# A hybrid encoder layer: the first token mixer's softmax is divided by its sums after the value product instead of before

## The chip, the cores and the metric

The kernel runs on one core of a Trainium2 chip. The metric is the device time of one execution in microseconds (us). Five engines of the core work side by side, each with its own instruction stream: TensorE (PE; the loading of its stationary operand is listed as PEld), VectorE (DVE), ScalarE (ACT), GpSimd (POOL) and SyncE (SP), which here only issues DMAs. 16 DMA engines move data between HBM and the on-chip SBUF. PSUM, where the matrix products land, has eight banks of 128 x 512 float32.

## The reference

One encoder layer on a sequence of 512 tokens of width 1024, everything in float32:

```
proj  = h @ w_in                                   # queries, keys, values of both mixers
o_a   = windowed_gqa_sink(qa, ka, va, a_sink)      # mixer A: 16 query heads, 4 key heads, |i-j| <= 128
o_b   = dilated_mixture(qb, kb, vb)                # mixer B: 3 groups (window, dilation) x 4 heads
g_a, g_b = split(sigmoid(h @ w_gate + b_gate))
mixed = g_a * (o_a @ w_br_a) + g_b * (o_b @ w_br_b)
h     = layer_norm(alpha * h + mixed @ w_out)
f     = (silu(h @ w_ff_gate) * (h @ w_ff_up)) @ w_ff_down
h     = layer_norm(alpha * h + f)
```

What matters here is mixer A. For each block of 128 queries and each head, with a learned logit `sk` beside the scores:

```
m   = max(sc.max(-1), sk)
p   = exp(sc - m)
den = p.sum(-1) + exp(sk - m)
o   = (p @ v) / den
```

The division by `den` may come before or after the product with `v`; the result is the same up to rounding.

## The kernel before

**Numbers as pairs.** A float32 operand is split into a rounded high part (a float32r copy) and a low part (the difference). A product of two split operands takes three matmuls: high by high, high by low, low by high. The high part is made by a copy on ACT or DVE (`copy`, line 387 on ACT, line 389 on DVE), the low part by a subtraction on DVE (mostly lines 413 and 558).

**Weights.** All weight matrices are packed into "units" of 128 x 1024, fetched as two halves of 128 x 512 (256 KB) into SBUF slots, mostly by SP (line 395). A unit that is used alone (`unit`, two calls of `half_unit`) takes 8 x 3 matmuls with 512 moving columns (`feat_k`, lines 537 to 539). Two units can be computed together by `pair_x`: seven products of half size in place of eight, by sums and differences of the weight halves (`S1` to `S4`) and of the input (`x_forms`). Each product is 12 matmuls with 256 moving columns (`product`, lines 659 to 661). Two of the sums of a pair (`S1`, `S3`) are made by a second DMA of POOL that adds into the first (line 401), two (`S2`, `S4`) on DVE, or by a DMA when the pair is written `D:`. The kernel before has 13 pairs.

**Scheduling.** The program is written as a list of operations with priorities. A planner inside the kernel (`Program.run`) plays the engines forward with costs of its own, and issues for each engine the ready operation with the lowest priority number whose buffers fit. So the order of the instructions on each engine is fixed when the program is built; on the chip, semaphores keep the dependencies and every engine works its list in order. The string `ORDER` names the steps of the first half: `X` the forms of the input, `q2` or `k1` a unit of queries or keys of mixer A, `VA` its values, `P:a,b` and `D:a,b` a pair, `R` and `r` the rotary turn of the rows waiting for it, `A0` to `A3` the four key heads of mixer A, `V0`, `V12`, `Q..`, `K..` and `B0` to `B3` the parts of mixer B, `g` a gate unit, `O` the fetch of one eighth of mixer A's result. The number behind `@` moves a step's priorities earlier (negative) or later.

**Mixer A.** `unit_a(g, b, ...)` does one key head `g` and one block `b` of queries, four heads at a time, 16 calls in all. For each head: two matmuls for the scores (lines 903 and 904), mask and maximum on DVE (line 1067), the exponential on ACT with the sum of the row (line 1071). Then DVE takes the reciprocal of the four sums (line 1074), and `normalise` multiplies each head's probabilities, 128 queries x 256 or 384 keys, by the reciprocal of its row: on ACT (line 1006) or on DVE (line 1008), whichever the planner has free. The probabilities are transposed by PE (line 1018) and multiplied with the values (lines 1084 and 1085). The result, head channels as rows and queries as columns, is stored to DRAM (`oaD`, line 1091) as two parts that must be added.

**The way back.** `fetch_oa(k)` (lines 1371 and 1372) loads the first part by SP and adds the second part by a POOL DMA, and `split_of` splits the sum (lines 1351 and 1357). There are eight such tiles; the first four put their high part in a slot, the others in a buffer of the class `x4` that has held the input (`N_XA = 4`).

**The branch stage.** After the steps of `ORDER`, a fixed list `BRANCHES` gives the order of eight products with `w_br_a` (`branch_a`, 24 matmuls each) and eight with `w_br_b` (`branch_b`). Then come the product with `w_out` (lines 1549 to 1551) with the first layer norm, the feed-forward part (lines 1759 to 1761 and 1970 to 1972) and the last layer norm.

Of the kernel before, what the change touches and what calls it, by code (L numbers as in the profile page):

```python
# [52 lines left out]
SPARE, SPARE2 = (4, 12)  # L53
# [48 lines left out]
PAIR_DMA = ()  # L102


BRANCHES = "a0 a1 a2 a3 a4 b0 a5 b1 b2 a6 b3 b4 a7 b5 b6 b7"
# [32 lines left out]
class Program:  # L138


    def __init__(self, limits):
# [7 lines left out]
        self.rooms = {}  # L149
# [5 lines left out]
    def op(self, alts, fn, reads=(), writes=(), prio=0.0, after=(), abs_prio=None, moves=0.0, extra=0, table=None):  # L155
# [30 lines left out]
        return o  # L186

# [19 lines left out]
    def run(self):  # L207
# [27 lines left out]
        while n_left:  # L235
# [13 lines left out]
            while progress:  # L249
                progress = False  # L250
                for e in engines:
# [19 lines left out]
                    for b in o.bufs:  # L271
                        if b.tile is None:
                            if b.keys[0] in self.rooms:
                                b.room = self.rooms[b.keys[0]].popleft()
# [70 lines left out]
def hybrid_layer(ctx: ExitStack, tc: tile.TileContext, wpack, xT, xtok, sink, bgate,  # L345
# [146 lines left out]
    for j in range(2):  # L492
        for w, u in (("k", U_KA), ("q", U_QA), ("v", U_VA), *((i, U_GATE + 8 + i) for i in range(N_ALONG))):
# [114 lines left out]
    def pair_x(ua, ub, by_dma=False):  # L608
# [3 lines left out]
        W, A = {}, {}  # L612

# [145 lines left out]
    def in_sbuf(u):  # L759

        ps, t = bank("dense"), slot()
        feat_x(ps, unit(u))
# [286 lines left out]
    obT = [slot(F32, "res") for _ in range(2)]  # L1049

    def unit_a(g, b, qs, kk, vs):
# [6 lines left out]
        for h in range(4):  # L1058
# [15 lines left out]
        op([(DVE, 0.08)], lambda e: nc.vector.reciprocal(st.t[:, 8:12], st.t[:, 4:8]),  # L1074
           reads=[(st, "l", h) for h in range(4)], writes=[(st, "r")])
        for h in range(4):
            normalise(lambda h=h: ps_[h].t[:, :n], ps_[h], n, lambda h=h: st.t[:, 8 + h:9 + h], (st, "r"))
# [205 lines left out]
    def gate_of(f, t):  # L1283
# [3 lines left out]
        if f in AWAY:  # L1287
            put_away(f)
# [6 lines left out]
    def gate(f, ps=None):  # L1295
# [8 lines left out]
        if f in AWAY:  # L1304
# [11 lines left out]

    psk, psq, psv = bank("dense"), bank("dense"), bank("dense")
# [12 lines left out]
    for f in range(N_ALONG):  # L1330
        gate(8 + f, ps=along[f])
    ka, qa = {0: k_near(psk, 4)}, {0: q_near(psq, 4, (0, 0))}
# [782 lines left out]
```

## Time and profile before

| | us |
|---|---|
| median of three runs | 724.5 (724.41 to 724.72) |
| the profiled execution | 724.82, of which 723.0 are the span of the instructions |
| PE busy | 712.5 |
| PEld busy | 667.2 |
| DVE busy | 664.4 |
| ACT busy | 494.6 |
| POOL busy | 173.2 |

The granted clock of TensorE is full speed all through. By the lines of PE's matmuls, the first products (five units beside each other, then one alone) run from 4 to 37 us, mixer A's scores appear from 64 to 236 us, mixer B's from 235 to 309 us, the branch stage begins at 301 us, the product with `w_out` at 362 us and the feed-forward part at 406 us. The last matmul ends at 716 us. PE's busy time overlaps in itself, since matmuls are pipelined: what one matmul costs is read from the distance of the starts.

### The profile page before, as it was taken

To read this page: it belongs to the slowest core of one execution; us is meant where nothing else is said; L and a number is where in the kernel's file an instruction comes from. 1 tells how busy PE (TensorE), PEld (TensorE's weight loads), DVE (VectorE), ACT (ScalarE), POOL (GpSimd) and SP (SyncE) were. 2 spreads that over 40 slices of the span, in tenths; PEclk is the share of its full clock that TensorE was granted. 3 is DMA by queue.
4 is the path that set the end of the run, shared out by engine and by line. 5 is a ranking of instruction groups with operands and counts; after the bars stand their busy time and mean duration, and the time that the engine had idled before them with its cause. 6 is when DMAs were issued, how large, how long until landed. Compare 5 with 4: busy or idle time off the path is not lost.

```text
span 723.0 us, 14810 instructions
## 1 busy us (share of the span) xinstructions
PE 712.5 (99%) x4947; PEld 667.2 (92%) x4947; DVE 664.4 (92%) x1425; ACT 494.6 (68%) x1136; POOL 173.2 (24%) x347
## 2 busy tenths in 40 slices
PE   8999999999999999999999999999999999999996
PEld 6889999998999998988888999999999999999985
DVE  6998999999999989999958998999999999999987
ACT  5768889889878997767625666756567566666821
POOL 0113343322423591550020022121121201212000
PEclk9999999999999999999999999999999999999999
DMA  8978967887568789766690499776897868979402
GB/s 257 294 215 210 235 168 213 227 216 179 137 169 204 187 255 253 219 196 219 199 210 33 110 300 232 177 203 165 238 238 197 223 164 219 253 196 194 106 29 88
DMA packets 81275, 141.44 MB, mean 196 GB/s; under 512 B 11024, under 2 KB 15760, under 8 KB 81200
## 3 DMA queue, kind: packets, MB, share of 16 engines
q1 hardware_dynamic: 63472, 107.07, 46.3%
q0 software_dynamic: 17456, 33.30, 26.6%
q8 instruction: 39, 0.64, 0.4%
q14 instruction: 36, 0.29, 0.1%
q10 hardware_dynamic: 272, 0.13, 0.1%
HBM read 119.69 MB, written 8.39 MB: 177 GB/s over the span
## 4 chain that ended last, share of the span: by engine, by line
PE 90%; DMA 4%; DVE 3%; SPq 2%; ACT 1%; issue 0%; POOL 0%; DVEq 0%; ACTq 0%; POOLq 0%
PE ps L1761 10%; PE ps L1759 10%; PE ps L1760 9%; PE ps L659 5%; PE ps L661 5%; PE ps L660 5%; PE ps L537 4%; PE ps L538 4%; PE ps L539 4%; PE ps L1970 4%; PE ps L1972 4%; PE ps L1971 4%; PE ps L1018 3%; DMA sl<-wpack 3%; PE ps L1549 3%; PE ps L1551 3%
## 5 line engine op out<-in xcount | busy, mean ns | idle before, releaser
L387 ACT ACTIVATE sl<-sl 128x512 fp32r<-128x512 f32 (+3 forms) x457 | 253.8, 588 | 60.7 <-DVE sl L558 43.3
L558 DVE TENSOR_TENSOR sl<-sl,sl 128x512 fp32r<-128x512 f32 (+3 forms) x415 | 245.3, 628 | 6.0 <-ACT sl L387 5.0
L387 ACT ACTIVATE sl<-ps 128x256 f32<-128x256 f32 (+6 forms) x214 | 88.5, 440 | 76.6 <-PE ps L1761 53.0
L401 POOL DMA_DIRECT2D sl<-wpack x70 | 63.0, 931 | 319.1 <-DMA sl<-wpack 92.0
L1760 PE MATMUL ps<-sl,sl 128*128 128x256 f32 x352 | 96.8, 275 | 0.0
L1761 PE MATMUL ps<-sl,sl 128*128 128x256 f32 x352 | 96.8, 275 | 0.0
L1759 PE MATMUL ps<-sl,sl 128*128 128x256 f32 x352 | 96.8, 275 | 0.0
L1759 PE MATMUL ps<-x,sl 128*128 128x256 f32 x264 | 72.6, 275 | 0.0
L1760 PE MATMUL ps<-x,sl 128*128 128x256 f32 x264 | 72.6, 275 | 0.0
L1761 PE MATMUL ps<-x,sl 128*128 128x256 f32 x264 | 72.6, 275 | 0.0
L1759 PEld LDWEIGHTS ps<-sl,sl 128*128 128x128 f32 x352 | 67.6, 192 | 0.1
L1760 PEld LDWEIGHTS ps<-sl,sl 128*128 128x128 f32 x352 | 67.6, 192 | 0.1
L1761 PEld LDWEIGHTS ps<-sl,sl 128*128 128x128 f32 x352 | 67.6, 192 | 0.0
L537 PE MATMUL ps<-x,sl 128*128 128x512 f32 (+1 forms) x161 | 62.1, 386 | 0.7 <-ACT x L387 0.7
L539 PE MATMUL ps<-x,sl 128*128 128x512 f32 (+1 forms) x161 | 60.9, 378 | 0.0
L659 PE MATMUL ps<-sl,sl 128*128 128x256 f32 x208 | 57.8, 278 | 0.9 <-ACT sl L667 0.9
L661 PE MATMUL ps<-sl,sl 128*128 128x256 f32 x208 | 57.3, 276 | 0.0
L660 PE MATMUL ps<-sl,sl 128*128 128x256 f32 x208 | 57.2, 275 | 0.0
L558 DVE TENSOR_TENSOR sl<-sl,ps 128x512 f32<-128x512 f32 (+1 forms) x72 | 47.3, 661 | 9.0 <-PE ps L1972 5.8
L1759 PEld LDWEIGHTS ps<-x,sl 128*128 128x128 f32 x264 | 50.6, 192 | 0.4
L1760 PEld LDWEIGHTS ps<-x,sl 128*128 128x128 f32 x264 | 50.6, 192 | 0.4
L1761 PEld LDWEIGHTS ps<-x,sl 128*128 128x128 f32 x264 | 50.7, 192 | 0.0
(174 smaller groups left out, 2006.6 us busy)
## 6 DMA issues: line engine op xcount, KB each, us to landing
sl<-wpack SPq DMA_DIRECT2D x254, 256.0 KB
sl<-wpack POOLq DMA_DIRECT2D x70, 256.0 KB, 5.5
wf<-wpack SPq DMA_DIRECT2D x51, 256.0 KB
sl<-sl SPq DMA_DIRECT2D x56, 128.0 KB
wf<-wpack POOLq DMA_DIRECT2D x24, 256.0 KB, 5.3
oa<-sl POOLq DMA_DIRECT2D x32, 128.0 KB, 3.6
sl<-sl SPq DMA_DIRECT2D x72, 32.0 KB
gz<-sl SPq DMA_DIRECT2D x8, 256.0 KB
```

The lines of the kernel that those rows point to most:

```text
L387: nc.scalar.activation(dst, src, AF.Copy)
L401: op([(POOL, 1.0)], lambda e: nc.gpsimd.dma_start(b.t, src2, accum_op=ALU.add), reads=[b], writes=[b], prio=prio, moves=1.65)
L537: mm(o, a, x0, start=(k == 0 and begins), stop=False, skip_group_check=split)
L538: mm(o, a, x1, start=False, stop=False, skip_group_check=split)
L539: mm(o, b, x0, start=False, stop=(k == nk - 1), skip_group_check=split)
L558: op([(DVE, dve(w))], lambda e: nc.vector.tensor_tensor(dst(), x(), y(), op=o), reads=reads, writes=writes, prio=prio)
L659: mm(o, wh, pairs(bh[k]()), start=(first and k == 0), stop=False, skip_group_check=True)
L660: mm(o, wh, pairs(bl[k]()), start=False, stop=False, skip_group_check=True)
L661: mm(o, wl, pairs(bh[k]()), start=False, stop=(k == 3), skip_group_check=True)
L1759: mm(o, wh, pairs(bh[k]()), start=(first and k == 0), stop=False, skip_group_check=True)
L1760: mm(o, wh, pairs(bl[k]()), start=False, stop=False, skip_group_check=True)
L1761: mm(o, wl, pairs(bh[k]()), start=False, stop=(k == 3), skip_group_check=True)
```

## The change

- In `unit_a` the reciprocals go into one tile `rall` (128 x 64: 16 columns for each block, four for each key head), and the four `normalise` operations are gone. The probabilities go on unnormalised.
- `sums_in_rows`, called by the first `O`, transposes `rall` with PE, four transposes of 128 x 16, so that each of the 16 heads becomes a row of 512 queries; copies the 16 rows out of PSUM and stores them to DRAM (`rD`).
- `fetch_oa` loads for each of its tiles two of these rows, each spread over 64 partitions by its DMA, into a slot `fac`, and multiplies the fetched tile by it on DVE before the split.
- `ORDER` has one more pair (`P:g,g`), 14 in all, for two gate units that were computed alone. The steps are in another order with other numbers; the first query and key units' rotation (`q0`, `k0`), which followed the first products directly, and the branch products (`a0` to `b7`, behind the mark `/`) are now steps of it. `BRANCHES` is gone.
- All eight high parts of `fetch_oa` go into slots (`N_XA = 8`). Some offsets change (`FORMS`, `VAL`, `OA_AFTER`, the reserve `SPARE`), and banks of PSUM for the class `d` are chosen by what they held before (`room_for`).
- `BY_DMA` and `PAIR_DMA`, lists of weight halves whose low part a DMA makes, get entries.

```diff
-SPARE, SPARE2 = (4, 12)
+SPARE, SPARE2 = (8, 12)
...
 ORDER = """
-X@-11 VA@-23 q2@-799 q1@-877 P:q3,g@-124 R@-106 D:k1,q4@-31 R@155 P:q5,Q01@-843 A0@-168 D:q6,q7@-47 D:g,g@-34 r@631 P:g,Q00@-22 L@-4 A2@-96
-D:g,K00@-31 A1@-48 R@187 V12@-20 P:g,K01@-67 R@-5 P:Q02,K02@-28 A3@-55 V0@55 R@5 B0@-7 B1@11 O@25 O@35 P:K10,Q10@-39 O@-13 O@-54 K11@-34 R@24
-O@11 P:Q12,Q11@-30 g@28 K12@-12 O@950 g@25 r O@43 P:g,g@-2 B2@-525 O@-304 B3@21 g@-29 P:g,g@-32 g@-8
+q0@-19 q1@-890 X@-157 P:q3,g@-307 R@78 k0@-34 D:k1,q4@-107 R@-5 VA@-216 q2@-427 A0@-228 P:q5,Q01@-811 D:q6,q7@-199 r@1495 D:g,g@-109
+P:g,Q00@-48 L@-92 D:g,K00@-19 A1@-71 V12@-11 R@-15 A3@-63 P:g,K01@-97 R@-22 A2@-343 P:Q02,K02@-13 r@-291 V0@25 B0@-44 O@-320 P:K10,Q10@-13
+K11@-37 O@-29 B1@-2 R@532 O@9 O@31 P:Q12,Q11@-8 P:g,g@-7 K12@-35 P:g,g@-24 O@-546 r g@-24 O@-7 B2@-572 O@-29 B3@-377 P:g,g@-42 O g@4 /@49
+a3@-30 a0@-14 a1@-22 a2@-53 b0@11 a4@-50 a5@-26 a6@8 b3@14 b1@-67 b2@-31 b4@38 a7@-39 b7@-16 b6@33 b5
 """
-FORMS = -255.0
-VAL = 140.0
-OA_AFTER = (1, 0, 0, 0, 0, 1, 0, 0)
+FORMS = -315.0
+VAL = 110.0
+OA_AFTER = (0, 0, 0, 1, 0, 0, 0, 0)
...
-STORE, OA, OA_SPLIT, OB_SPLIT, N_OA, N_XA = 0.0, -60.0, -140.0, -140.0, 4, 4
+STORE, OA, OA_SPLIT, OB_SPLIT, N_OA, N_XA = 0.0, -60.0, -140.0, -140.0, 4, 8
-BY_DMA = ()
+BY_DMA = [(14, 1), (31, 0), (38, 0), (45, 1), (64, 1)]
-PAIR_DMA = ()
+PAIR_DMA = [(15, 'A12')]
-BRANCHES = "a0 a1 a2 a3 a4 b0 a5 b1 b2 a6 b3 b4 a7 b5 b6 b7"
+GATES = (8, 9, 10, 11, 12, 13, 14, 15, 0, 1, 2, 3, 4, 5, 6, 7)
...
+    def room_for(self, b):
+        free = self.rooms[b.keys[0]]
+        if b.keys[0] != "bank":
+            return free.popleft()
+        room = next((r for r in free if self.whole.get(r)), free[0]) if b.keys[1] == "d" else free[0]
+        free.remove(room)
+        self.whole[room] = b.keys[1] in ("dense", "o", "d", "dff")
+        return room
...
     def half_unit(u, j):
-        if j == 1 and u in BY_DMA:
+        if (u, j) in BY_DMA:
...
+        nth = env["pairs"]
+        env["pairs"] += 1
...
-            if key in PAIR_DMA:
+            if (nth, key) in PAIR_DMA:
...
+    rall = fixed([P, 64], "rall")
+    rD = Buf("dram", None, lambda: dram.tile([16, S], F32, name=name("rD")))
+
+    def sums_in_rows():
+        pb, rows = bank("tb"), slot()
+        def go(e):
+            for b in range(NR):
+                nc.tensor.transpose(pb.t[0:16, b * P:(b + 1) * P], rall.t[:, 16 * b:16 * b + 16], ident.t)
+        op([(PE, 0.436)], go, reads=[ident, *[(rall, g, b) for g in range(4) for b in range(NR)]], writes=[pb])
+        op(cp_alts(S, True), lambda e: copy(e, rows.t[0:16], pb.t[0:16]), reads=[pb], writes=[rows])
+        op([(SP, 0.1)], lambda e: nc.sync.dma_start(rD.t, rows.t[0:16]), reads=[rows], writes=[rD])
+        env["rows"] = True
...
     def unit_a(g, b, qs, kk, vs):
-        op([(DVE, 0.08)], lambda e: nc.vector.reciprocal(st.t[:, 8:12], st.t[:, 4:8]),
-           reads=[(st, "l", h) for h in range(4)], writes=[(st, "r")])
-        for h in range(4):
-            normalise(lambda h=h: ps_[h].t[:, :n], ps_[h], n, lambda h=h: st.t[:, 8 + h:9 + h], (st, "r"))
+        c = 16 * b + 4 * g
+        op([(DVE, 0.08)], lambda e: nc.vector.reciprocal(rall.t[:, c:c + 4], st.t[:, 4:8]),
+           reads=[(st, "l", h) for h in range(4)], writes=[(rall, g, b)])
...
-    ka, qa = {0: k_near(psk, 4)}, {0: q_near(psq, 4, (0, 0))}
+    ka, qa = {}, {}
...
     def fetch_oa(k):
+        if "rows" not in env:
+            sums_in_rows()
...
+        fac = slot()
+        for i in range(2):
+            op([(SP, 0.365)], lambda e, i=i: nc.sync.dma_start(
+                fac.t[64 * i:64 * i + 64], rD.t[2 * k + i].partition_broadcast(64)), reads=[rD], writes=[(fac, i)], prio=OAP[k // 4])
+        op([(DVE, dve(S))], lambda e: nc.vector.tensor_tensor(st.t, st.t, fac.t, op=ALU.mult),
+           reads=[st, (fac, 0), (fac, 1)], writes=[st], prio=OA_SPLIT)
...
     def step(w):
+        elif w == "/":
+            late()
+        elif w[0] in "ab":
+            branch(w)
+        elif w in first_of:
+            first_of[w][1](first_of[w][0], False)
...
-    sa.extend(fetch_oa(k) for k in range(len(sa), 8))
-    MA = moving(sa)
+    def late():
+        op([(POOL, 0.0)], free_all, after=lasts)
+        sa.extend(fetch_oa(k) for k in range(len(sa), 8))
+        MA.extend(moving(sa))
+        env["late"] = True
```

More of the change, by code (lines that the diff above doesn't have):

```diff
@@ L1286, in gate_of @@
             t.t, t.t, AF.Tanh, bias=bg.t[:, f:f + 1], scale=0.5), reads=[(t, 1), (t, 2), bg], writes=[t], prio=EV)
-        if f in AWAY:
+        if f in AWAY and not env["late"]:
             put_away(f)
@@ L1303, in gate @@
            reads=[ps, bg], writes=[t], prio=EV)
-        if f in AWAY:
+        if f in AWAY and not env["late"]:
             put_away(f)
@@ L1315, in dense_k @@
         return k_post(ps, nt) if nt else k_pairs(ps)
+    env = {"pairs": 0, "gate": N_ALONG, "turn": [], "qs": {}, "ks": {}, "late": False}
     psk, psq, psv = bank("dense"), bank("dense"), bank("dense")
@@ L1449, in step @@
                 op([(POOL, 0.0)], lambda e: pr.limits.update(ROOMS[hs]), after=list(exps))
-    for w in ORDER.split():
-        w, _, later = w.partition("@")
-        pr.T += float(later or 0)
-        step(w)
-        pr.T -= float(later or 0)
     def free_all(e):
@@ L1459, in free_all @@
         pr.spare = SPARE2
-    op([(POOL, 0.0)], free_all, after=lasts)
     def moving(parts):
@@ L1507, in branch_b @@
         return mark
-    names = BRANCHES.split()
-    marks = []
-    for n, w in enumerate(names):
-        k = 8 + int(w[1])
-        if w[0] == "b":
-            if k in away:
-                fetch_gate(k, [*exps, marks[names.index("b%d" % (k - 11))]] if k > 10 else exps)
-        marks.append((branch_a if w[0] == "a" else branch_b)(int(w[1])))
-    for w, mark in zip(names, marks):
-        env[w] = [mark]
+    for w in ORDER.split():
+        w, _, later = w.partition("@")
+        pr.T += float(later or 0)
+        step(w)
+        pr.T -= float(later or 0)
     xt = {(t, j): slot() for t in range(NR) for j in range(2)}
```

47 lines of the change are left out of this document (31 added, 16 removed).

## The prediction

> **What bounds the kernel now.** I read the page's busy times first, then PE's waits, then the starts of single matmuls.
>
> ```profile
> span 723.0 us, 14810 instructions
> ...
> PE 712.5 (99%) x4947; PEld 667.2 (92%) x4947; DVE 664.4 (92%) x1425; ACT 494.6 (68%) x1136; POOL 173.2 (24%) x347
> ...
> q1 hardware_dynamic: 63472, 107.07, 46.3%
> q0 software_dynamic: 17456, 33.30, 26.6%
> ```
> ```profile
> PE ps L473 <- DVE eps L524: 1.2, 1, 1.2
> PE ps L659 <- ACT sl L667: 0.9, 1, 0.9
> PE ps L537 <- ACT x L387: 0.7, 1, 0.7
> PE ps L1018 <- ACT sl L1006: 0.4, 1, 0.4
> ```
>
> PE waits four times, 3.2 us in all. The first and third waits (1.2 + 0.7) are the start of the program, which the diff leaves alone. What an edit of the first half can win by removing waits is 0.9 + 0.4 = 1.3 us; all else must come from fewer or shorter matmuls. The timeline gives the price of a matmul, first and last row of two undisturbed stretches:
>
> ```profile
> 364.66 0.38 PE L1551 MATMUL ps<-sl,sl 128*128 128x512 f32 x1
> ...
> 372.00 0.38 PE L1549 MATMUL ps<-sl,sl 128*128 128x512 f32 x1
> ```
> ```profile
> 424.78 0.28 PE L1761 MATMUL ps<-sl,sl 128*128 128x256 f32 x1
> ...
> 431.93 0.28 PE L1759 MATMUL ps<-sl,sl 128*128 128x256 f32 x1
> ```
>
> 35 rows, 34 steps: 7.34 / 34 = 0.216 us for 512 columns. 65 rows, 64 steps: 7.15 / 64 = 0.1117 us for 256 columns. The tail behind the last matmul is the last layer norm, which the change doesn't touch.
>
> **The change on PE.** One more pair: 7 x 12 x 0.1117 = 9.38 us in place of two units of 24 matmuls, 48 x 0.216 = 10.37 us: -0.99 us. The other 13 pairs are there before. The reciprocals' transposes are four, and the identity streams 128 columns in each, as in mixer A's own transposes, of which the chain of waits shows eight in a row:
>
> ```profile
> 85.44 0.87 PE ps L1018 x8
> ```
>
> 4 x 0.87 / 8 = +0.44 us. Sum on PE: -0.55 us. Order on PE costs nothing as long as nothing is waited for.
>
> Against the pair speaks a rule of the Trainium skill (Perfetto Trace Analysis, section Identifying the Most-Contended Engine): matmul busy time is a poor measure of headroom, and the busy share of the weight loads is to be used. A pair has 84 loads in place of 48. If loads set the pace, the pair would lose, which is the last rival below. The steps of 0.1117 us, each with its own load, speak against it here.
>
> **What falls away on ACT and DVE.** The normalising of mixer A, 32 instructions of 384 and 32 of 256 columns; the 256 rows hold 24 of mixer B too, which stay:
>
> ```profile
> L1006 ACT ACTIVATE sl<-sl,st 128x256 f32<-128x256 f32 x32 | 14.6, 497 | 2.2 <-DVE st L1074 2.2
> L1006 ACT ACTIVATE sl<-sl,st 128x384 f32<-128x384 f32 x19 | 10.7, 609 | 0.0
> L1008 DVE TENSOR_SCALAR sl<-sl,st 128x256 f32<-128x256 f32 x24 | 7.7, 348 | 0.1
> L1008 DVE TENSOR_SCALAR sl<-sl,st 128x384 f32<-128x384 f32 x13 | 5.4, 431 | 0.1
> L558 DVE TENSOR_TENSOR sl<-sl,sl 128x512 f32<-128x512 f32 x66 | 45.0, 685 | 0.5
> ```
>
> With 32 of 56 shared as the whole is, ACT loses 19 x 0.609 + 18 x 0.497 = 20.5 us and DVE 13 x 0.431 + 14 x 0.348 = 10.5 us, all between 64 and 236 us. PE has no wait in that stretch (the 0.9 comes at 42 us, the 0.4 at 279 us), so I cost this relief at nothing; its cover is PE's own queue of matmuls. The reciprocals stay, 16 as before.
>
> **What is added later.** Eight multiplications of 128 x 512 on DVE, 8 x 0.685 = 5.5 us, and the pair's extra splits: seven weight tiles in place of four and two sums, 5 x 0.685 = 3.4 us. These 8.9 us fall mainly into 250 to 340 us, where `O` and the pairs of gates stand in `ORDER`. DMA gets 16 loads of 128 KB, which is 2.1 MB. By the page's queue rows a plain MB costs 0.463 x 723 / 107.07 = 3.1 us of all 16 engines, an added-up MB 0.266 x 723 / 33.30 = 5.8 us. So the rows cost 6.6 us, and the pair (five plain loads for four and two adding ones, 0.26 MB each) 0.8 + 3.0 = 3.8 us. The windows of that stretch (PE, PEld, DVE, ACT, POOL busy, clock, DMA share, GB/s):
>
> ```profile
> 250.00:300.00 50.00, 49.60 (x331) 45.57 (x330) 44.37 (x113) 39.30 (x106) 25.35 (x69) 1.00 0.91 241
> 300.00:340.00 40.00, 40.00 (x225) 35.98 (x224) 37.25 (x103) 28.67 (x74) 16.51 (x63) 1.00 0.65 210
> ```
>
> DVE has 90 - 81.6 = 8.4 us free in these 90, DMA 50 x 0.09 + 40 x 0.35 = 4.5 + 14 = 18.5. The additions fit or nearly so if the order spreads them, so I take 0. Ends: -0.4 us (PE's fourth wait, at 279 us, goes) and +5.9 us (the DMA rival).
>
> SP gets 17 more issues, and each waits in its list: the loads of the rows for the one store of `rD`, behind which queue the weight loads that SP issues next. The nearest row for such a trip through DRAM is a 128 KB store, 3.6 us from issue to landing. Weight tiles loaded ahead cover it; without them PE would wait those 3.6 us, less than the DMA rival's 5.9. POOL gets the pair's two adding DMAs; it is busy 25.35 of 50 and 16.51 of 40 us there, so 0. The copy of the 16 rows out of PSUM is one instruction on ACT, which has 22 us free in these 90.
>
> ```profile
> oa<-sl POOLq DMA_DIRECT2D x32, 128.0 KB, 3.6
> ```
>
> **The first pair's wait.** The chain of waits leading to the 0.9 us:
>
> ```profile
> 34.81 0.63 DVE sl L558
> 35.45 0.72 DVE sl L774
> 36.17 0.57 DVE sl L772
> 36.74 1.20 DVE sl L558 x2
> 37.94 0.54 DVE sl L772
> 38.48 0.73 DVE sl L774
> 39.20 0.56 DVE sl L558
> 39.77 0.60 DVE sl L776
> 40.37 0.61 DVE sl L558
> 41.07 0.65 ACT sl L387
> ...
> 43.13 0.28 ACT sl L667
> ```
>
> Lines 772 to 776 rotate the first query and key units. They stand before the forms that the pair needs, 3.2 of DVE's 6.2 us; ACT waits for the last form, with the eviction of line 667 behind it in its list, and PE waits for that. In the change `q0` and `k0` are steps of their own, `k0` behind a pair, and the forms are more urgent (`FORMS` and `X`). The same forms, the same loads and the same in-order lists remain, though, and a second pair is pulled nearer. Ends: -0.9 (gone) and +0.9 (twice). As half of DVE's stretch is the rotation, I take half the wait: -0.45.
>
> **Edits at no cost.** The new entries of `BY_DMA` and `PAIR_DMA` reach nothing: units 14, 31 and 45 are computed in pairs, 38 in the first products, 64 in the feed-forward part, none by `half_unit`; and pairs count from 0 to 13, so there is no 15. The four high parts moved into slots no longer wait for the input's buffers; PE has no wait where those are read (40.00 busy of 40 from 300 on), so 0, and if the eight slots of rows and four of parts crowd out loads, it is the DMA rival again. The choice of banks and the order of the branches fall where PE shows no wait either: 0.
>
> **Sum.** 724.8 (the profiled execution) - 0.55 - 0.45 = 723.8. The profiled one lies 0.3 above the median of the three runs, so 723.5 by the median.
>
> **The rivals.** 0.2%, about what a measurement of this kernel can tell from no change, is 1.45 us: under 723.05 is faster, over 725.95 slower.
>
> *Both waits go and none comes:* -0.55 - 0.9 - 0.4 = -1.85, so 722.6, or a little lower with the small starts of PE's switches. For it: the relief before 236 us leaves room to prepare the later pairs early. Against: the wait at 279 us is for line 1006 of mixer B, which stays.
>
> *DMA is late at the fetches (slower):* from 250 to 300 us 4.5 us are free, and 6.6 + 3.8 = 10.4 us of transfers come in. If nothing of it moves behind 300 us, 5.9 us stay over, and branch products or the last pairs wait for rows or weights. It decides from 0.55 us seen by PE on, where the gain of the pair is spent; half of the overflow is +3.0: 724.5 - 0.55 + 3.0 = 727.0. For it: the chain to the wait at 279 us already begins with a fetch, `oa`, of 6.4 us, and a row move behind it.
>
> ```profile
> 261.01 6.40 DMA sl<-oa
> 267.43 3.51 DMA sl<-sl
> ```
>
> Against: those 14 us from 300 on, and `fetch_oa` may start after `B0` rather than `B1`.
>
> *DVE becomes the bound from 250 to 340 us:* 8.9 us against 8.4 free is an overflow of 0.5; with the first wait unchanged 724.5 - 0.55 + 0.5 = 724.4.
>
> *Weight loads set the pace:* the pair costs 84 x 0.192 = 16.1 us by PEld's durations, 5.8 above the 10.37, so 724.5 + 5.8 + 0.4 = 730.7.
>
> ```profile
> L661 PEld LDWEIGHTS ps<-sl,sl 128*128 128x128 f32 x208 | 39.9, 192 | 0.1
> ```
>
> **How the numbers follow.** The sum of small terms (half the first wait) 0.33, both waits gone 0.36, DVE 0.13, DMA 0.16, weight loads 0.02. The first and third stay within 0.2%, less some spread to either side; the second is faster; the last two are slower. That gives 0.38 faster, 0.44 the same, 0.18 slower. Low end: 722.3, the second case with a start or two less. High end: 726.0, into the DMA case (1.5 us seen by PE), leaving about one in ten above it.
>
> **What would show it.** Lines 659 to 661 with 392 matmuls each rather than 364, spaced as before, and four transposes more. Lines 1006 and 1008 with 32 instructions left in all, those of mixer B. PE's list of waits without the 0.9 or with it halved. In the windows from 250 to 340 us, DMA near full before 300 and DVE near full throughout; PE under its 49.60 and 40.00 would speak for the DMA or the DVE rival, and its releaser tells which. A multiplication waiting long for its row, with branch matmuls behind it, would make the prediction wrong; so would a wait of several us anywhere in the first 340.

## The result, and the profile after

| | median, us | ratio to before, 95% interval |
|---|---|---|
| before, 20 executions beside the change | 724.71 (723.97 to 725.79) | |
| changed, 20 executions | 731.57 (726.46 to 739.27) | 1.0086 (1.0067 to 1.0106) |

Two of the 20 executions (738.34 and 739.27 us) are in a slow state; without them the median is 731.08 us, and the ratios and all comparisons below leave such executions out. The change makes the kernel slower by 0.9%; by these medians it is 6.4 us. The prediction, 723.5 in a range of 722.3 to 726.0, missed. The kernel before repeats within 1.8 us; the other 18 executions of the changed one spread over 8.6 us. The profiled execution of the changed kernel is the quickest of its 20 (726.46 us), so its page shows the least of what went wrong, and I read a second profile of the same kernel (732.31 us) beside it.

The page of the changed kernel: span, busy times, DMA queues, and the shares of the chain that ended last.

```profile
span 724.6 us, 14933 instructions
...
PE 713.0 (98%) x4987; PEld 668.1 (92%) x4987; DVE 662.1 (91%) x1406; ACT 485.8 (67%) x1112; POOL 167.6 (23%) x349
...
q1 hardware_dynamic: 65056, 109.60, 48.1%
q0 software_dynamic: 17744, 33.83, 26.8%
...
PE 84%; DMA 7%; DVE 4%; SPq 2%; ACT 2%; issue 1%; POOL 0%; DVEq 0%; ACTq 0%
```

ACT has 8.8 us less to do and DVE 2.3 us less, and the time is longer all the same: neither was what PE waited for. DMA's share of the chain is now 7% (4% before). PE's waits (line waited at, what it waited for, us in total, times, longest):

```profile
PE ps L483 <- DVE eps L534: 1.2, 1, 1.2
PE ps L1280 <- DVE sl L978: 1.1, 1, 1.1
PE ps L671 <- ACT sl L679: 1.0, 2, 0.6
PE ps L1677 <- DVE sl L1659: 0.6, 1, 0.6
PE ps L1237 <- ACT sl L1020: 0.2, 1, 0.2
```

The lines have moved by 10 to 47: 671 is the pairs' product (659 before), 1020 the normalising on ACT, now of mixer B alone (1006), 1677 the transposes behind the first layer norm. New are the second row, a product of mixer B (line 1280) that waits for the split of its values (line 978), the fourth, and the small fifth. The two windows that the prediction quoted, now of the changed kernel (us, busy PE, PEld, DVE, ACT, POOL, clock, DMA share, GB/s):

```profile
250.00:300.00 50.00, 48.62 (x334) 44.81 (x334) 46.30 (x104) 39.58 (x93) 18.12 (x37) 1.00 0.94 249
300.00:340.00 40.00, 40.00 (x231) 36.11 (x230) 36.99 (x108) 28.90 (x80) 17.23 (x68) 1.00 0.75 226
```

PE lost 1.4 us before 300, and DMA is busier there, 0.94 against 0.91. Where the 1.1 us come from is in the chain of waits (start, us, what):

```profile
266.56 8.72 DMA sl<-wpack
275.30 0.54 SPq L766
275.88 3.86 DMA sl<-sl
...
281.70 6.02 DMA sl<-wpack
287.74 0.63 ACT sl L397
...
290.77 0.61 ACT sl L397
...
293.07 0.60 DVE sl L1410
...
294.28 0.34 DVE sl L978
294.75 0.75 PE ps L1280 x4
```

The chain follows a weight load (`wpack`) of 8.7 us, a rotary move of SP, and another weight load of 6.0 us. Then ACT makes high parts one after another, DVE has the multiplication by the rows (line 1410) and the split of mixer B's values behind them, and PE waits for that split. The first weight load of the chain has this ahead of it in SP's list (timeline of SP, start, us):

```profile
235.20 2.45 SPq L1408 DMA_DIRECT2D sl<-rD  x4
...
238.81 0.45 SPq L1408 DMA_DIRECT2D sl<-rD  x1
...
239.94 1.09 SPq L1408 DMA_DIRECT2D sl<-rD  x2
...
241.71 1.08 SPq L1408 DMA_DIRECT2D sl<-rD  x2
...
243.48 0.44 SPq L1408 DMA_DIRECT2D sl<-rD  x1
...
259.04 5.52 SPq L1408 DMA_DIRECT2D sl<-rD  x6
...
266.00 0.97 SPq L405 DMA_DIRECT2D sl<-wpack  x2
```

Line 1408 is the row load. A row of this view runs from the start of its first issue to the end of its last, so the sixteen take up 2.45 + 0.45 + 1.09 + 1.08 + 0.44 + 5.52 = 11.0 us of SP's list. 8.0 us of it are the issues themselves, 0.44 to 0.59 us each; the rest is waiting between them, 2.6 us in the row of the last six alone. The weight load at 266.0 is the next load of weights behind them.

What the issues wait for is in SP's own waits, from 230 to 310 us:

```profile
SPq L856 <- DMA sl<-wpack: 5.0, 5, 1.6
SPq L766 <- DMA sl<-wpack: 1.8, 1, 1.8
...
SPq L1408 <- DMA sl<-wpack: 1.6, 2, 1.0
```

A row load reads nothing of a weight load. But in the trace the 569 DMAs of SP report their landing by eight semaphores in fixed turn, and 554 of them wait, before they are issued, for the semaphore that they are to use. So an issue stands still until the DMA eight issues ahead of it has landed: the last six row loads wait in this way for three weight loads and one fetch, 2.4 us.

The second profile of the same kernel, 732.31 us, has the same wait, longer; its waits, and its windows at the place:

```profile
PE ps L1280 <- DVE sl L978: 3.7, 1, 3.7
```
```profile
280.00:300.00 20.00, 16.27 (x100) 14.51 (x99) 16.47 (x35) 14.38 (x33) 3.48 (x4) 1.00 0.87 242
300.00:340.00 40.00, 40.00 (x215) 35.72 (x214) 35.24 (x104) 26.10 (x72) 17.25 (x68) 0.96 0.77 228
```

PE stands still for 3.7 us, and after that the granted clock is 0.96 over 40 us, 1.6 us more. Over the 18 executions the mean clock falls from 0.998 (726.46 us) to 0.992 (735.07 us); (1 - clock) x time grows from 1.5 to 5.9 us, so by this estimate some 4.4 of the 8.6 us of spread are clock, and the rest would be the waiting itself.

### The profile page after: what moved, and what is told of

Same layout as the page of the kernel before. It is cut to its first block, busy times and chain, and to the rows that moved or that the text cites. A ratio compares the mean times of both kernels' runs of the same rounds, so it can differ in the third digit from the quotient of the medians.

```text
span 724.6 us, 14933 instructions
## 1 busy us (share of the span) xinstructions
PE 713.0 (98%) x4987; PEld 668.1 (92%) x4987; DVE 662.1 (91%) x1406; ACT 485.8 (67%) x1112; POOL 167.6 (23%) x349
## 4 chain that ended last, share of the span: by engine, by line
PE 84%; DMA 7%; DVE 4%; SPq 2%; ACT 2%; issue 1%; POOL 0%; DVEq 0%; ACTq 0%
PE ps L1807 10%; PE ps L1808 9%; PE ps L1806 9%; DMA sl<-wpack 5%; PE ps L671 4%; PE ps L672 4%; PE ps L673 4%; PE ps L2017 4%; PE ps L2019 4%; PE ps L2018 4%; PE ps L547 3%; PE ps L549 3%; PE ps L548 3%; PE ps L1032 3%; PE ps L1598 3%; PE ps L1596 3%
## 5 line engine op out<-in xcount | busy, mean ns | idle before, releaser
L397 ACT ACTIVATE sl<-sl 128x512 fp32r<-128x512 f32 (+3 forms) x468 | 259.2, 589 | 57.7 <-DVE sl L568 35.3
L568 DVE TENSOR_TENSOR sl<-sl,sl 128x512 fp32r<-128x512 f32 (+3 forms) x424 | 252.2, 629 | 8.0 <-ACT sl L397 7.0
L397 ACT ACTIVATE sl<-ps 128x256 f32<-128x256 f32 (+7 forms) x215 | 89.8, 440 | 78.1 <-PE ps L1808 50.7
L411 POOL DMA_DIRECT2D sl<-wpack x72 | 66.1, 938 | 312.5 <-DMA sl<-wpack 84.9
L1807 PE MATMUL ps<-sl,sl 128*128 128x256 f32 x352 | 96.8, 275 | 0.0
L1808 PE MATMUL ps<-sl,sl 128*128 128x256 f32 x352 | 96.8, 275 | 0.0
L1806 PE MATMUL ps<-sl,sl 128*128 128x256 f32 x352 | 96.8, 275 | 0.0
L671 PE MATMUL ps<-sl,sl 128*128 128x256 f32 x224 | 62.3, 278 | 1.0 <-ACT sl L679 1.0
L672 PE MATMUL ps<-sl,sl 128*128 128x256 f32 x224 | 61.6, 275 | 0.0
L673 PE MATMUL ps<-sl,sl 128*128 128x256 f32 x224 | 61.6, 275 | 0.0
L423 DVE TENSOR_TENSOR sl<-sl,sl 128x512 fp32r<-128x512 f32 x70 | 46.6, 682 | 2.4 <-ACT sl L397 2.4
L2017 PE MATMUL ps<-sl,sl 128*128 128x512 f32 x126 | 47.8, 380 | 0.0
```

The source lines that it names most:

```text
L397: nc.scalar.activation(dst, src, AF.Copy)
L411: op([(POOL, 1.0)], lambda e: nc.gpsimd.dma_start(b.t, src2, accum_op=ALU.add), reads=[b], writes=[b], prio=prio, moves=1.65)
L423: op([(DVE, dve(S))], lambda e: nc.vector.tensor_tensor(l.t, src.t, f32(h.t), op=ALU.subtract), reads=[src, h], writes=[l], prio=prio, abs ...
L568: op([(DVE, dve(w))], lambda e: nc.vector.tensor_tensor(dst(), x(), y(), op=o), reads=reads, writes=writes, prio=prio)
L671: mm(o, wh, pairs(bh[k]()), start=(first and k == 0), stop=False, skip_group_check=True)
L672: mm(o, wh, pairs(bl[k]()), start=False, stop=False, skip_group_check=True)
```

## The experiments

Theory A, the rival of the prediction: the sixteen row loads make DMA late between 240 and 300 us, by their bytes (2.1 MB). Theory B: the new order itself is at fault. Theory C came up on the way: the number of issues is the price, whatever they move. In the table "row loads" are those of line 1408; each ratio is to the kernel before on the same chip at the same time. The kernels without row loads, with short rows and with loads from the weights do not compute the layer: mixer A's factors are left out or wrong in them.

| kernel | row loads | median, us | before, us | ratio, 95% interval |
|---|---|---|---|---|
| changed, a second time | 16 of 128 KB | 731.24 | 724.72 | 1.0080 (1.0055 to 1.0105) |
| no row loads | none | 725.81 | 724.72 | 1.0016 (1.0003 to 1.0030) |
| short rows | 16 of 4 KB | 727.60 | 724.50 | 1.0046 (1.0018 to 1.0075) |
| from the weights, one row repeated | 16 of 128 KB | 729.18 | 724.50 | 1.0069 (1.0043 to 1.0095) |
| from the weights, plain | 16 of 128 KB | 731.08 | 724.50 | 1.0098 (1.0070 to 1.0126) |
| the same, every second partition | 16 of 128 KB | 731.82 | 724.49 | 1.0096 (1.0079 to 1.0113) |
| from the weights, one load a tile | 8 of 256 KB | 726.40 | 724.43 | 1.0023 (1.0011 to 1.0036) |
| the change with one load a tile | 8 of 256 KB | 727.04 | 724.49 | 1.0036 (1.0023 to 1.0049) |
| the same, issued by POOL | 8 of 256 KB | 728.73 | 724.43 | 1.0063 (1.0051 to 1.0076) |
| the change, loads issued by ACT | 16 of 128 KB | 733.36 | 724.27 | 1.0125 (1.0106 to 1.0144) |
| before, with 16 extra copies | 16 copies of 128 KB | 729.25 | 724.27 | 1.0068 (1.0052 to 1.0084) |
| before, with 16 short copies | 16 copies of 4 KB | 728.48 | 724.43 | 1.0057 (1.0045 to 1.0070) |

Below, "over before" is the median less that of the kernel before in the same row, and two kernels are compared by it.

### The changed kernel again, twice

> The changed kernel as it is, once more, for a profile of another execution: the one shown (726.5 us) is the fastest of its executions, the median is 731.6 us. Row theory (the fetches with their 16 row loads make DMA late from 240 to 300 us): an execution near 731 us shows PE waits of some 4 to 6 us more in 240 to 300 us than the fast one, the releasers ending in landings of weights or of the result's fetch. Order theory (the new order of the first steps leaves too little time for landings, the rows are innocent): the additional waits lie before 240 us, above all at 40 to 65 us.

> The changed kernel once more, for the profile of another execution (median 731.6 us, from 726.5 to 739.3). Traffic theory: where the execution is some us slower than the 726.5 us shown, PE's additional waits lie between 240 and 340 us, with landings of DMAs in the chain before them, and a wait near 3 us or more is followed by a lower granted clock. Order theory: they lie at 40 to 65 us and at 400 us.

731.24 us, 6.5 over before, against 731.08 at first; the single execution gave 732.31 and the second profile shown above. The loss comes back. The profile of the first of these two runs is of its quickest execution (727.43 us), and the wait at line 1280 is 0.3 us there, so it shows little of the loss.

### Without the row loads

```diff
-            op([(SP, 0.365)], lambda e, i=i: nc.sync.dma_start(
-                fac.t[64 * i:64 * i + 64], rD.t[2 * k + i].partition_broadcast(64)), ...
+            op([(SP, 0.365)], lambda e, i=i: None, ...
-        ... nc.vector.tensor_tensor(st.t, st.t, fac.t, op=ALU.mult)
+        ... nc.vector.tensor_tensor(st.t, st.t, st.t, op=ALU.mult)
```

> The changed kernel with the same instruction order, but without the 16 row loads of fetch_oa; the fetched tile is multiplied with itself, so the results of mixer A are left out of their scale. Row theory: 2.1 MB less (6.6 us of all DMA engines) in the stretch where DMA is full; the median falls to 724 to 726 us and the spread shrinks to about 2 us. Order theory: the median stays at 729 to 732 us with a spread of several us.

1.1 us over before, where the change is 6.4: 5.3 us are gone with the order and all multiplications left as they are. Its window has no gap left:

```profile
250.00:300.00 50.00, 50.00 (x350) 46.73 (x349) 47.38 (x107) 40.91 (x96) 17.89 (x35) 1.00 0.92 235
```

So the row loads are most of the price, and the multiplications on DVE are not. The remaining 0.16% over the kernel before belong to the rest of the change, the new order above all; no run takes them apart.

### One part of the change alone

The factors in rows alone, in the order and numbers of before:

> The kernel before with mixer A's part of the change alone: no normalising, reciprocals into rows, row loads and multiplications at the fetch; the planner still leaves the room of the normalising, so the order of the first 230 us is that of before, 13 pairs. PE gains 0.44 us of work. Row theory: 727 to 731 us and a spread of several us, since the rows meet the same full DMA. Order theory: 724.5 to 726 us with the narrow spread of before.

744.61 us, ratio 1.0273 (1.0253 to 1.0294). The pair alone:

```diff
-... g@28 K12@-12 O@950 g@25 r ...
+... P:g,g@-7 K12@-12 O@950 r ...
```

> The kernel before with its order string changed in one place: two gate units behind the dilated pair are computed as a pair (14 pairs). PE's work falls by 0.99 us. Row theory: 723.5 to 725 us, narrow spread (the pair brings 3.8 us of DMA, less than the rows). Order theory: the same or anything up to 728 us, as every new plan may be late at landings.

737.41 us, ratio 1.0174 (1.0147 to 1.0200); this program's outputs are not the layer's, so its time counts for less still. Neither part tells its own price this way. With an edited list of steps the planner lays out another program, and new waits come in many places (2.5, 1.8, 1.6 and 1.6 us in the first, 3.3 and 2.2 us in the second) that neither kernel has. The same showed when I moved one number of the changed kernel, to have the values of mixer B split earlier:

```diff
-... V0@25 ...
+... V0@-30 ...
```

> The changed kernel with one number of the order string changed, V0@25 to V0@-30: the values of mixer B's first group, for whose product PE waits longest (up to 3.9 us at 294 us), are prepared earlier; the plan from some 100 us on is another one. If the lateness belongs to that one step: 727 to 729 us, and no wait of PE at the window product. If the stretch as a whole has too little DMA time: the wait comes back elsewhere between 240 and 340 us, 730 to 740 us.

753.79 us, ratio 1.0413 (1.0391 to 1.0434). The waits at line 1280 came to 0.9 us, and longer ones stand elsewhere, 5.2 us at line 671 and 4.6 us at line 917.

From here on I changed only the transfers and kept the order of PE, ACT and DVE.

### What of the row loads costs: bytes, source, repeated reading

```diff
-                fac.t[64 * i:64 * i + 64], rD.t[2 * k + i].partition_broadcast(64)), ...
-        ... nc.vector.tensor_tensor(st.t, st.t, fac.t, op=ALU.mult), ...
+                fac.t[64 * i:64 * i + 64, 0:16], rD.t[2 * k + i, 0:16].partition_broadcast(64)), ...
+        ... nc.vector.tensor_tensor(st.t[:, 0:S], st.t[:, 0:S], st.t[:, 0:S], op=ALU.mult), ...
```

> The changed kernel with the same instruction order and the same 16 row loads on SP, each cut to 16 of 512 columns (64 partitions x 64 bytes); the fetched tile is multiplied with itself, so mixer A's scale is left out. Traffic theory (the 2.1 MB fill the DMA engines): as without the row loads, 725 to 727 us. Issue theory (16 more issues hold SP's list, and what stands behind them is late): still 729 to 732 us. Wait theory (the loads wait for the store of the rows and hold SP's list): still 729 to 732 us.

3.1 us over before. Of the 5.3 us that the row loads cost, 3.3 are gone without the bytes and 2.0 stay, though the interval overlaps that of the kernel without row loads. A profiled wait of 1.2 us at line 1280 stays too.

```diff
+                fac.t[64 * i:64 * i + 64], wpack[U_BRA + k, 64 * i:64 * i + 64, 0:S]), ...
```

> The changed kernel with the same instruction order, the 16 row loads replaced by loads of the same size from 64 different rows of a weight matrix, which wait for nothing; mixer A's scale is wrong by that. Traffic and issue theory: 729 to 733 us as with the rows. Row theory in the narrow sense (64 reads of one row just written are slow) and wait theory: 725 to 727 us.

6.6 us over before: as slow as the change, from other memory, with 64 different rows and with nothing to wait for in `rD`.

```diff
+                fac.t[64 * i:64 * i + 64], wpack[U_BRA + k, 64 * i, 0:S].partition_broadcast(64)), ...
```

> The changed kernel with the same instruction order, the 16 row loads read one row of a weight matrix 64 times each, with no wait for the stored reciprocals; mixer A's scale is wrong by that. If reading one row 64 times is what costs: 729 to 733 us while the plain loads are at 725 to 727. If the wait for the store costs: 725 to 727 us in both. Traffic and issue theory: 729 to 733 us in both.

4.7 us over before; its interval overlaps that of the plain loads and that of the change. So neither the trip through DRAM nor the reading of one row 64 times is the price. Up to here theory A stood.

### Does the old order bear the same traffic?

```diff
+    ballast = [dram.tile([P, S], F32, name=name("ballast")) for k in range(8)]
...
+        def fetch(e):
+            for i in range(2):
+                nc.sync.dma_start(ballast[k][64 * i:64 * i + 64], wpack[U_BRA + k, 64 * i:64 * i + 64, 0:S])
+            nc.sync.dma_start(st.t, src(0))
...
+        op([(SP, 0.73)], fetch, ...
```

> The kernel before, its instruction order unchanged, with 16 extra copies of 128 KB as pure ballast: two ahead of each of the eight fetches on SP, from a weight matrix to a scratch place in DRAM; the outputs are computed as before. Traffic and issue theory (the stretch from 250 to 300 us has no DMA and SP time to spare, in the old order too): 728 to 735 us and a spread of several us. Order theory (only the new order is so tight that it notices): 724.5 to 726 us, narrow.

5.0 us over before, in the unchanged order. Its window and its longest wait:

```profile
250.00:300.00 50.00, 46.73 (x304) 42.22 (x303) 39.67 (x93) 34.84 (x90) 23.38 (x65) 0.97 0.95 258
```
```profile
PE ps L1018 <- ACT sl L1006: 3.2, 2, 1.8
```

Theory B falls as the main cause: the old order has no room for sixteen more transfers either, and it loses at the very wait, line 1018 for line 1006, of 0.4 us that the prediction quoted.

### Another engine's list

```diff
-            op([(SP, 0.365)], lambda e, i=i: nc.sync.dma_start(
+            op([(SP, 0.365)], lambda e, i=i: nc.scalar.dma_start(
```

> The changed kernel with the same computation and the same place of each instruction in the plan, but the 16 row loads are issued by ACT instead of SP. With the row loads at 731.7 us, cut to 64 bytes a partition at 727.6 and left out at 725.8: if the issues on SP cost the difference of the last two, 1.8 us, this lies near 729.5 to 730.5; if they cost nothing and the bytes all, near 731.5. If ACT's list is held by the issues (16 more instructions that wait), slower than 732.

9.1 us over before, not better. This run doesn't separate issues from bytes, since ACT's list now pays for the issues. The window at 260 us of the changed kernel, then of this one, where ACT (the fourth of the busy times) is held:

```profile
260.00:270.00 10.00, 9.71 (x81) 9.18 (x80) 9.02 (x25) 9.01 (x26) 5.54 (x9) 1.00 1.07 262
```
```profile
260.00:270.00 10.00, 7.73 (x67) 7.45 (x65) 4.94 (x16) 4.10 (x13) 5.31 (x8) 1.00 1.05 270
```

It does show what an issue can cost. In ACT's timeline one row load stands still until an earlier row load, the last user of the same semaphore, lands at 269.75 us, and ACT's next copy behind it has been held for 4.6 us; at 272.6 us PE has waited 4.8 us:

```profile
269.77 0.45 ACTq L1408 DMA_DIRECT2D sl<-rD  x1
270.27 0.63 ACT L397 ACTIVATE sl<-sl 128x512 fp32r<-128x512 f32 x1 [4.62 <-DMA sl<-rD]
```
```profile
PE ps L1237 <- DVE sl L1057: 4.8, 1, 4.8
```

### Half the issues, the same bytes

```diff
+            op([(SP, 0.365)], lambda e, i=i: None if i else nc.sync.dma_start(
+                fac.t, wpack[U_BRA + k, :, 0:S]), ...
```

> The changed kernel with the two row loads of a tile (64 partitions, 128 KB each) replaced by one load of 256 KB over all 128 partitions, from the weights instead of rD, issued where the first of the two stood; the multiplication takes that tile, so the result is not the layer's. Same bytes as with sixteen plain loads (731.08 us), half the issues on SP, and no load that reaches only half of the partitions. Theory of bytes (the 2.1 MB are the price, whatever their form): 730 to 731.5, a wait of about 2 us at 293 us stays. Rival, the form is the price (the Trainium skill, DMA: Bandwidth & Descriptors, table of what to do, advises one transfer over 128 partitions in place of two to halves): then half or more of the 5.3 us over the kernel without row loads (725.81) goes, 726.5 to 728.5, and the wait at 293 us is under 1 us.

2.0 us over before, against 6.6 with the same bytes in sixteen loads: theory A, by bytes alone, falls. PE's waits of this kernel, and the issues on SP, from a profile of its quickest execution (723.55 us):

```profile
PE ps L483 <- DVE eps L534: 1.2, 1, 1.2
PE ps L1677 <- DVE sl L1659: 0.6, 1, 0.6
PE ps L548 <- DVE x L520: 0.2, 1, 0.2
```
```profile
234.01 1.20 SPq L1408 DMA_DIRECT2D sl<-wpack  x2
236.22 0.42 SPq L1408 DMA_DIRECT2D sl<-wpack  x1
237.22 0.39 SPq L1408 DMA_DIRECT2D sl<-wpack  x1
238.74 0.33 SPq L1408 DMA_DIRECT2D sl<-wpack  x1
257.25 2.43 SPq L1408 DMA_DIRECT2D sl<-wpack  x3
```

The wait at line 1280 is gone. The eight issues take up 4.8 us of SP's list, the changed kernel's sixteen 11.0.

The Trainium skill (DMA: Bandwidth & Descriptors, section Rules for kernel authors) advises one transfer over 128 partitions in place of two to disjoint halves. The 4.6 us agree. The page gives as reason that the halves share the same DMA engines, and whether the halves as such matter is the next run.

```diff
+                fac.t[i:128:2], wpack[U_BRA + k, i:128:2, 0:S]), ...
```

> As the kernel with sixteen plain loads from the weights (731.08 us), but load i of a tile fills the partitions i, i + 2, i + 4 and so on in place of one half: same count of issues, same bytes, same 2 KB rows; the factors are the wrong numbers. Theory of the halves (a load to 64 neighbouring partitions holds only part of the ways into the memory, and what is behind it waits): as with eight loads, 726 to 727.5. Theory of the issues (sixteen issues on SP push back the weight loads): 730 to 732, with a wait of 2 us at 293 us.

7.3 us over before: with every second partition of all 128 it is as slow as with halves. Which partitions a load reaches does not matter here; how many loads there are does.

### The change itself with eight row loads

```diff
-    rall = fixed([P, 64], "rall")
+    rall = fixed([P, 512], "rall")
...
-                nc.tensor.transpose(pb.t[0:16, b * P:(b + 1) * P], rall.t[:, 16 * b:16 * b + 16], ident.t)
+                nc.tensor.transpose(pb.t[:, b * P:(b + 1) * P], rall.t[:, P * b:P * b + P], ident.t)
...
-        op([(DVE, 0.08)], lambda e: nc.vector.reciprocal(rall.t[:, c:c + 4], st.t[:, 4:8]),
+        op([(DVE, 0.08)], lambda e: nc.vector.reciprocal(rall.t[:, c:c + 32]..., st.t[:, 4:8].unsqueeze(2).broadcast_to([P, 4, 8])),
...
+            op([(SP, 0.365)], lambda e, i=i: None if i else nc.sync.dma_start(
+                fac.t, rD.t[16 * k:16 * k + 16].unsqueeze(1).broadcast_to([16, 8, S])), ...
```

> The changed kernel with the same result, but one row load a tile: each reciprocal is written eight times into rall, the four transposes give 128 rows in place of 16, rD is 128 x 512 (256 KB stored in place of 32), and a tile's factors come by one load of 16 rows, each read eight times, over all 128 partitions. Bytes of loads as in the change, eight issues in place of sixteen. If the form is the price in the change too: 726 to 728, the changed kernel's 731.6 less some 4 us. If the price is that of the rows' trip through DRAM or of their repeated reading: 730 to 732.

2.6 us over before: the same computation as the change, with 3.8 us of its 6.4 given back. It beats the changed kernel and still loses 0.36% to the kernel before; by its median no kernel here beats that one. The profile is of its slowest execution (729.93 us), and it too has no wait at line 1280. Its longest wait, 3.2 us, stands at 58 us, long before the first row load at 239 us, so what is left of the loss need not be the row loads':

```profile
PE ps L671 <- ACT sl L679: 3.5, 2, 3.2
```

```diff
-            ... nc.sync.dma_start(fac.t, rD.t[16 * k:16 * k + 16]...
+            ... nc.gpsimd.dma_start(fac.t, rD.t[16 * k:16 * k + 16]...
```

> The changed kernel with one row load of 128 partitions a tile, same result, the eight loads issued by POOL instead of SP. Theory of SP's list (an issue costs since weight loads stand behind it on SP): 725.5 to 726.5, what the kernel without row loads takes (725.81), since POOL is busy only 18 of 50 us between 250 and 300. Theory of the transfers (each costs the DMA engines its share wherever it is issued): 727 or more, as with SP (727.04).

4.3 us over before: taking the eight issues out of SP's list does not help, it costs. POOL's list has the adding DMAs in it, so this doesn't free the issues either: it cannot tell SP's list from POOL's, or both from what the transfers take.

The Trainium skill (DMA: Bandwidth & Descriptors, section Issuing engines are not separate DMA queues) has it that starting DMAs from several engines saves only sequencer time, usually small beside the transfer. That the move to ACT or POOL gains nothing agrees. Small beside the transfer holds for one issue, 0.50 us on the mean of the sixteen beside 3.7 us from issue to landing of a 128 KB store in the same trace; it leaves out what stands behind an issue that waits.

### Issues without bytes in the old order

```diff
-                nc.sync.dma_start(ballast[k][64 * i:64 * i + 64], wpack[U_BRA + k, 64 * i:64 * i + 64, 0:S])
+                nc.sync.dma_start(ballast[k][64 * i:64 * i + 64, 0:16], wpack[U_BRA + k, 64 * i:64 * i + 64, 0:16])
```

> The kernel before with sixteen extra copies ahead of its fetches on SP, as in the run with ballast (729.25), but 64 rows of 64 bytes each in place of 2 KB. Theory of SP's list: 728 to 729.5, as with the whole copies. Theory of the transfers' bytes: 724.5 to 725.5, the kernel before's time. Between them: both count.

4.1 us over before: sixteen issues that move 64 KB in all cost nearly what they cost with 2.1 MB (5.0; the intervals overlap). Here SP's list itself stands in the chain of waits:

```profile
260.23 0.58 SPq L1374
260.98 0.46 SPq L1375
261.48 0.50 SPq L1374
262.02 2.04 DMA ballast<-wpack
```

Line 1374 is the extra copy, line 1375 the fetch. No instruction reads the copy, so the chain's step through its landing is an inference of the profile. In the order of before, theory C holds: the issues are the price, and their bytes add little.

### What the runs settle

The number of DMA issues between 235 and 265 us carries most of the loss: eight in place of sixteen give back 3.8 us in the change and 4.6 us in the kernel with plain loads. In the new order the bytes count beside it: over the kernel without row loads, sixteen issues nearly without bytes cost 2.0 us, eight with all bytes 0.9 and 1.5, sixteen with all bytes 3.6 to 6.2. That reads like a reserve of a few us that either alone stays nearly within and both together exceed.

The traces show a candidate for it. From 230 to 300 us, SP's issues wait for the landing of the DMA eight issues before them for 1.2 us in the kernel before; for 13.2 to 15.4 us in the six profiles with sixteen whole loads on SP in the new order; and for 9.1 to 10.8 us in that order with eight loads, with sixteen short ones, with the loads moved to POOL and with none. The copies in the old order raise it to 6.8 us, the short copies to 5.0. Both halves of the result fit it. Sixteen plain loads of 128 KB land after 5.2 us on the median and eight of 256 KB after 5.3, so a load cut in two takes two of the eight places for as long as the whole one takes one; and the short rows land after 3.4 us, those of the change after 4.8. No run changes the number of places, so that this wait sets the loss is shown for the one issue on ACT and argued for the rest. What each transfer itself takes from the DMA engines stays open.

## Why the prediction was wrong, point by point

**The additions, costed at 0: the step that failed.** "SP gets 17 more issues, and each waits in its list ... Weight tiles loaded ahead cover it". I priced this as one trip of 3.6 us that is covered, and not as sixteen places in a list that has eight DMAs on their way at most. In the timeline they take up 11.0 us of SP, the weight loads come behind them, and PE waits for what those feed; without the row loads 5.3 us are gone. The planner does not have this wait: it counts 0.7 us of SP for an issue of line 1408 (0.365 is the transfer's share of DMA), which is close to the 0.69 that the trace shows with the waits, but it issues the next whether or not an earlier one has landed. The other half of the step, "The additions fit or nearly so if the order spreads them, so I take 0", compared the mean free share of DMA. Its upper end, +5.9 us, was near what the row loads cost (6.4 - 1.1 = 5.3), in part by luck, since it counted bytes alone; I took 0 because of the 14 us free after 300; the order does not put the loads there, the last six stand at 259 us.

**The rival "DMA is late at the fetches".** The direction was its, with 0.16 of chance; its price was 3.0 us where the row loads cost 5.3, and its cause was only half right. It counted bytes; the runs show the number of loads first. It expected branch products or late pairs to wait; the one that waits is mixer B's window product at 294 us, three queues away: weight load, ACT's list, DVE's list. What it named as its sign came: PE at 48.62 instead of 49.60 in 250 to 300, DMA share up to 0.94.

**PE's work, -0.55.** Right by count, and not refuted in time. The products have 392 matmuls a line, in two groups, 224 + 168:

```profile
L671 PE MATMUL ps<-sl,sl 128*128 128x256 f32 x224 | 62.3, 278 | 1.0 <-ACT sl L679 1.0
L671 PE MATMUL ps<-x,sl 128*128 128x256 f32 x168 | 46.9, 279 | 0.0
```

The distances between the starts of matmuls, without those in which PE waits, sum to 711.2 us after and 711.6 before, 0.3 less; since two more of them are left out after, this cannot tell the size of the gain.

**The first pair's wait, -0.45.** Wrong. It is now two waits of line 671 for line 679, 1.0 us together against 0.9 before. The second, at 55 us, is a pair pulled nearer, the upper end that I had named ("a second pair is pulled nearer") and not taken.

**Order on PE, and the branches, at 0.** Wrong by 0.6 us: the wait of line 1677 behind the first layer norm is in the change and, as line 1676, in the kernel without row loads, and not in the kernel before. It would be over half of the 1.1 us by which the kernel without row loads still loses; which edit brings it is not shown.

**The relief of ACT and DVE before 236 us, at 0.** Right: PE had no wait there to be shortened. Of the normalising 32 instructions are left, as forecast, 23 on ACT and 9 on DVE. That is why the change has no gain to set against its price but the pair's.

**DVE as the bound.** It did not come: 46.30 + 36.99 = 83.3 of 90 us busy, and without the row loads DVE did the same multiplications with PE at 50.00 of 50.

**Weight loads set the pace.** It did not come: PEld has the same 92%, and the pair's matmuls keep their 0.11 us. The rule of the Trainium skill that I had weighed (Perfetto Trace Analysis, section Identifying the Most-Contended Engine) cannot tell here whether loads or matmuls set PE's pace, since that share is the same before and after; the matmuls' steps can.

**Both waits go.** The wait at 279 us did go, with 0.2 us at line 1237 (267 us) for the same normalising in its place; the first didn't, and a longer one came.

**Not in the sum at all.** A wait of several us also lowers the granted clock, and a kernel whose transfers land late by chance has a wide spread: its median is not that of the one profile that happens to be quick.

## What to carry to other kernels

Price every added DMA twice, by its bytes and by its place in the in-order list that carries it, in the stretch where it stands; look in the trace for how many of a list's DMAs may be on their way at once (eight here). Two transfers that fill one tile should be one. Work taken off an engine that nobody waits for buys nothing, so it can't pay for transfers put into the one stretch that is full. Where executions of a kernel spread much more than before, read more than one profile: a quick execution hides the wait that sets the median.

## What the runs showed of the hardware that I had not expected

An issue on SP took the same time whether it moved 128 KB or 4 KB: 0.44 to 0.59 us for the sixteen whole rows, 0.44 to 0.60 us for the sixteen short ones but for one of 1.57. With the waits between them the last six short rows take up 6.03 us of SP, the last six whole ones 5.52.

The adding DMAs of the fetches took longer to land in the change, first its row, then that of the kernel before (issues, KB each, median us to landing). In the kernel without row loads they took 7.8 us, so about half of the difference comes with the new order and not with the row loads:

```profile
sl<-oa POOLq DMA_DIRECT2D x8, 256.0 KB, 9.2
```
```profile
sl<-oa POOLq DMA_DIRECT2D x8, 256.0 KB, 6.1
```

One long wait of PE can cost more than its length: after 3.7 us of standing still the granted clock was 0.96 over the next 40 us; taken by single microseconds it is 0.61, 0.50, 0.50 and 0.68 from 300 to 304 us and 1.00 around them. The Trainium skill (TensorE: Matmul & The Clock Gate, Part 1) says that the clock is halved after an idle window of about 3.4 us; 40 us at 0.96 is 3.2 us at half clock, which agrees. The length of one wait does not decide it here: after 3.2 us in the change with one load a tile (58 us) the clock stayed at 1.00, after 2.9 us with every second partition it went to 0.50, and the kernel before with sixteen extra copies had 0.97 between 250 and 300 us, with no wait of over 1.8 us.
